# Extra yields ahead of the merge products and the convolution's transposes in a two-layer hybrid encoder

## The chip, the cores and the metric

One core of one Trainium2 chip runs the whole program. The metric is the device time of one execution in microseconds. The kernel before took 2913.32 us, the median of three runs (2912.23 to 2919.48).

## What is computed

The program is a two-layer encoder. In each layer a normalised input of 1024 positions is multiplied by one wide matrix `w_in`, and the columns of the product feed three mixers:

- a convolution module: a gated product of two column groups (256 channels), a depthwise convolution along the sequence, a layer norm over the channels, SiLU;
- differential attention: two softmax maps of queries and keys, one subtracted from the other, applied to values;
- a gated delta rule in two directions: queries, keys and values behind a short convolution, with a decay and a step size for each position. It is computed in chunks of 64 positions. In each chunk a unit lower triangular 64x64 matrix A, made of keys and decays, has to be inverted.

The results are merged by an output projection, and a feed-forward block follows. All products are held to fp32 accuracy: an operand is split into a high and a low part, and three matmuls stand for one product.

## The kernel before

**The phase that the change touches** is `w_in_phase` (L293). It multiplies by `w_in` in 21 steps of 128 columns each. A step (`dense_fm`) loads one weight tile (the DMA L177 on SP's queue), splits it (L168 on ACT, L169 on DVE), issues 2 x 8 x 3 = 48 matmuls (L163, L164, L165: the high and low parts), and evacuates the product by a function of its own (L425 to L429 for queries and keys of the attention, L440 for its values and for z). Both layers run this phase, from about 90 us and from about 1500 us in the trace.

**Work laid among the steps.** Two Python generators are advanced between the steps; each `yield` ends a portion of issued instructions. Behind every step, `prep` is advanced 8 times; from the moment that both inputs of the convolution exist, `conv_module` is advanced 6 times. This goes on until 5 steps are left (`LATE`); behind that the rest of both generators is issued, and the last 5 steps alternate with the delta rule's own products.

- `conv_module` (L485): the depthwise convolution on DVE (L508, L512: products over 31 taps for two halves of the channels, into the tiles `ca`), then for each quarter q of the sequence the transposes of `ca` on TensorE (L525), the layer norm's statistics on DVE, a power on POOL (L158, `lnro`), L530 on DVE, transposes back (L534), and SiLU on ACT (L537).
- `prep`: for each of the three head pairs p, `dn_a(p)` makes the chunk matrices A (transposes L674 and L718, decays L704 and L708 on POOL, the product L723 on DVE). It is advanced one portion for every two portions of `invert(p-1)`. What is left of `invert(p-1)` follows before `invert(p)` exists. At the end `prep_v` (L642 to L646) runs beside `invert(2)`.
- `invert(p)` (L762): A is taken as four 32x32 blocks. It loads the diagonal blocks (tiles `Lr` and `Lp`, DMAs L776, a transposing copy L777 on ACT), inverts them by 31 substitution steps on POOL (L787, L788 on the tile `Xm`), transposes the result on ACT (L790, `XT`), stores both to DRAM (L792, L793 on SP), loads them back as `Tt` and `Ta` (L801, L804: 12 DMAs on SP), yields once, and then issues the products that merge the blocks: 32 with `Ta` (L811, L812), an evacuation (L814), 32 with `Tt` (L819, L820), the evacuations L823 and L824 and the store L826 into `kta`, from which the delta rule reads (L859). `Lr` and `XT` share one pair of buffers, so that `Lr` of pair p+1 is allocated behind `XT` of pair p.

**What sets the order.** Nothing in the source fixes the order on an engine. A planner simulates the program while it is being built: it places each instruction on its engine (and each DMA on its queue) when its inputs are ready in that simulation, and among ready ones it takes the one that was issued first. So the place at which an instruction is issued is a priority. Evacuations and weight loads are issued with a priority that is higher by 1000 instructions. One step, with the portions of the generators that go with it, issues some 110 instructions, so this is about 9 steps. What the planner has fixed is the order on the chip; an engine there waits at an instruction whose input is late, and everything behind it waits too.

Steps 0 to 3 are two tiles for the delta rule and the two inputs of the convolution (each of twice the length); 4 to 8 are further tiles of the delta rule, 9 to 14 the queries and keys of the attention (q0, k0, q1, k1, q2, k2), 15 to 17 its values, 18 to 20 z.

Of the kernel before, what the change touches and what calls it, by code (L numbers as in the profile page):

```python
# [78 lines left out]
class K:  # L79
# [403 lines left out]
    def conv_module(self, l, L, W, up, dw, db, lw, lb):  # L483
        nc = self.nc
        cas = []  # L485
        for i in range(2):
            ca = W.tile([P, S], F32, tag="ca", bufs=2, name=f"ca{l}_{i}")
            u = up[i]

            H, M = S // 2, S // 2 + 15  # L490
            xe, xo = u[:, 0::2], u[:, 1::2]
            ye, yo = ca[:, 0::2], ca[:, 1::2]
            h0, h1 = dw[:, i, 0::2], dw[:, i, 1::2]
            hs = W.tile([P, 16], F32, tag="hs", bufs=2, name=f"hs{l}_{i}")
            nc.vector.tensor_tensor(hs[:, 0:15], h0[:, 0:15], h1, op=ALU.add)
            nc.vector.tensor_copy(hs[:, 15:16], h0[:, 15:16])
            x1 = W.tile([P, M], F32, tag="x1", bufs=1, name=f"x1_{l}_{i}")
            nc.vector.tensor_tensor(x1[:, 0:M - 1], xe[:, 1:M], xo[:, 0:M - 1], op=ALU.subtract)
            nc.vector.tensor_tensor(xe, xe, xo, op=ALU.subtract)
            yield  # L500
            nc.vector.tensor_scalar(yo, xo[:, 0:H], hs[:, 0:1], db[:, i:i + 1], ALU.mult, ALU.add)
            for k in range(1, 16):
                nc.vector.scalar_tensor_tensor(yo, xo[:, k:k + H], hs[:, k:k + 1], yo, ALU.mult, ALU.add)
                if k % 2:
                    yield
            nc.vector.scalar_tensor_tensor(ye, xe[:, 0:H], h0[:, 0:1], yo, ALU.mult, ALU.add)
            for k in range(1, 16):
                nc.vector.scalar_tensor_tensor(ye, xe[:, k:k + H], h0[:, k:k + 1], ye, ALU.mult, ALU.add)  # L508
                if k % 2:
                    yield  # L510
            for k in range(15):
                nc.vector.scalar_tensor_tensor(yo, x1[:, k:k + H], h1[:, k:k + 1], yo, ALU.mult, ALU.add)  # L512
                if k % 2:
                    yield
            cas.append(ca)
        for q in range(4):
            ps = self.bank("sc0", 1).rearrange("p (t k) -> p t k", k=CONV_CH)
            pa = self.bank("sc1", 1).rearrange("p (i t k) -> p i t k", i=2, k=P)
            xc = W.tile([P, 2, CONV_CH], F32, tag="lnx", bufs=2, name=f"lnx{l}_{q}")
            st = W.tile([P, 2, 6], F32, tag="lnst", bufs=2, name=f"lnst{l}_{q}")  # L520
            mv = W.tile([P, 2, 2], F32, tag="lnmv", bufs=2, name=f"lnmv{l}_{q}")
            for tt in range(2):
                t = 2 * q + tt
                for i in range(2):
                    nc.tensor.transpose(ps[:, tt, i * P:(i + 1) * P], cas[i][:, t * P:(t + 1) * P], self.ident)  # L525
                nc.vector.bn_stats(st[:, tt], ps[:, tt])
                nc.vector.bn_aggr(mv[:, tt], st[:, tt])
            r = self.rstd(W, mv[:, :, 1], 1.0, 1e-5, "lnr")
            for tt in range(2):
                nc.vector.tensor_scalar(xc[:, tt], ps[:, tt], mv[:, tt, 0:1], r[:, tt:tt + 1], ALU.subtract, ALU.mult)  # L530
            yield
            for i in range(2):
                for tt in range(2):
                    nc.tensor.transpose(pa[:, i, tt], xc[:, tt, i * P:(i + 1) * P], self.ident)  # L534
            yo = W.tile([P, 2, CONV_CH], F32, tag="lnx", bufs=2, name=f"yo{l}_{q}")
            for i in range(2):
                nc.scalar.activation(yo[:, i], pa[:, i].rearrange("p t k -> p (t k)"), AF.Silu, scale=lw[:, i:i + 1], bias=lb[:, i:i + 1])  # L537
                nc.scalar.dma_start(self.yd[i, :, q * CONV_CH:(q + 1) * CONV_CH], yo[:, i])
            yield
# [218 lines left out]
    def invert(self, l, p, A, X):  # L758
# [39 lines left out]
        for g in range(4):  # L798
# [3 lines left out]
                                  xi[1 - d, 64 * d + 16 * g:64 * d + 16 * g + 16].rearrange("m r c -> r m c"))  # L802
            d = g % 2
            nc.sync.dma_start(Ta[r], xi[d, 64 * d + 16 * g:64 * d + 16 * g + 16].rearrange("m r c -> r m c"))  # L804
        yield
        ps = self.dt_bank().rearrange("p (g c) -> p g c", c=B)
        Tf = [t.rearrange("p m h c -> p (m h) c") for t in Tt]
        for g in range(16):
# [826 lines left out]
```

## Time and profile before

| | |
|---|---|
| median of three runs | 2913.32 us |
| the profiled execution | 2917.9 us |
| its span in the trace | 2916.1 us |
| mean granted TensorE clock | 0.956 of full speed |
| TensorE matmuls (PE), busy | 2681.5 us, 92% |
| VectorE (DVE), busy | 2064.0 us, 71% |
| ScalarE (ACT), busy | 1404.8 us, 48% |
| GpSimd (POOL), busy | 842.7 us, 29% |

The profile is one execution, taken by the hardware profiler. Its span is 1.8 us under its own time, and its time is 4.6 us over the median of the runs. Engines are PE (TensorE matmul), PEld (its weight loads), DVE, ACT, POOL and SP; SPq is the DMA queue that SP issues. A name such as L525 is a line of the kernel. A row of the timeline gives start and duration in us, engine, line, operation, output<-inputs and shape, and in brackets the idle time of the engine just before and what ended it. Busy shares are means over stages with different limits.

### The profile page before, as it was taken

The numbers are of one execution on the slowest core, as the hardware profiler recorded it, in microseconds if no ns is written. First come the engines' busy times: TensorE is split into PE (matmuls) and PEld (weight loads), VectorE is DVE, ScalarE is ACT, GpSimd is POOL, SyncE is SP. The second block draws the span as 40 slices with busy tenths as digits, with TensorE's granted clock in tenths as the row PEclk, the third lists the DMA queues.
The fourth block names the chain that finished last, engine by engine and source line by source line (L and its number), as shares of the span: only waits on it lengthen the run. The fifth ranks groups of instructions, "written<-read, shape, count | busy, mean of one in ns | idle before, by whom it ended". The sixth has DMA issues, their size and how long they took to land.

```text
span 2916.1 us, 46184 instructions
## 1 busy us (share of the span) xinstructions
PE 2681.5 (92%) x17292; PEld 2155.4 (74%) x17292; DVE 2064.0 (71%) x3781; ACT 1404.8 (48%) x2468; POOL 842.7 (29%) x793
## 2 busy tenths in 40 slices
PE   8987989888999998999999879698889999989997
PEld 7865766666888886888787667476668888868886
DVE  5797247987488776777768871388874977757776
ACT  5433336586356664322554332276853566643224
POOL 2289636754100000000112985377530000000000
PEclk9998989989999999999999989799989999999999
DMA  5467795433235558655445496953332455586643
GB/s 133 151 172 210 219 225 145 117 102 123 87 105 216 206 192 314 233 202 184 150 118 146 142 265 170 224 150 107 109 121 75 145 196 206 212 336 209 220 169 116
DMA packets 415314, 504.76 MB, mean 173 GB/s; under 512 B 125401, under 2 KB 313945, under 8 KB 412786
## 3 DMA queue, kind: packets, MB, share of 16 engines
q1 hardware_dynamic: 359362, 373.92, 42.9%
q10 hardware_dynamic: 55728, 127.88, 11.5%
q8 instruction: 137, 2.24, 0.3%
q14 instruction: 87, 0.71, 0.1%
HBM read 318.01 MB, written 182.12 MB: 172 GB/s over the span
## 4 chain that ended last, share of the span: by engine, by line
PE 62%; POOL 11%; DMA 10%; DVE 8%; issue 4%; ACT 2%; SPq 2%; ACTq 0%; DVEq 0%; POOLq 0%
PE at L163 10%; PE at L164 10%; PE at L165 10%; PE sc L163 4%; PE sc L164 4%; PE sc L165 4%; POOL Xm L788 4%; POOL subt L787 3%; DVE sc L1070 3%; PE dt L163 2%; PE dt L164 2%; PE dt L165 2%; PE tr L163 2%; PE tr L164 2%; DMA qkT<-gq 2%
## 5 line engine op out<-in xcount | busy, mean ns | idle before, releaser
L158 POOL TENSOR_TENSOR pro<-pr,mhalf 128x1 f32<-128x1 f32 x32 | 18.5, 578 | 1417.8 <-DVE pr L207 1415.0
L163 PE MATMUL at<-hTh,wh 128*128 128x512 f32 (+1 forms) x832 | 326.8, 394 | 11.8 <-DVE qkl L426 8.0
L165 PE MATMUL at<-hTh,wl 128*128 128x512 f32 (+1 forms) x832 | 325.5, 392 | 5.4 <-DVE wl L169 5.4
L164 PE MATMUL at<-hTl,wh 128*128 128x512 f32 (+1 forms) x832 | 326.3, 392 | 0.0
L1073 ACT ACTIVATE sc<-sc,mx 128x1024 f32<-128x1024 f32 x192 | 220.2, 1149 | 94.3 <-DVE mx L1070 89.1
L163 PEld LDWEIGHTS at<-hTh,wh 128*128 128x128 f32 x832 | 160.3, 193 | 43.4 <-DVE qkl L426 8.5
L165 PEld LDWEIGHTS at<-hTh,wl 128*128 128x128 f32 x832 | 160.3, 193 | 37.2 <-DVE wl L169 6.2
L164 PEld LDWEIGHTS at<-hTl,wh 128*128 128x128 f32 x832 | 160.6, 193 | 31.0 <-issue 0.8
L1068 PE MATMUL at<-stk 96*128 96x512 f32 x352 | 153.7, 489 | 29.7 <-DVE mx L1070 27.9
L1070 DVE CUSTOM_DVE_ANT_0 sc<-at,bias 128x512 f32<-128x512 f32 x192 | 129.7, 684 | 43.0 <-PE at L1068 25.0
L1070 DVE CUSTOM_DVE_ANT_0 sc<-at,bias,mx 128x512 f32<-128x512 f32 x192 | 141.9, 745 | 19.6 <-PE at L1068 13.8
L1180 ACT ACTIVATE ob<-sb 128x512 fp32r<-128x512 f32 x120 | 74.8, 626 | 155.0 <-PE tr L165 54.8
L169 DVE TENSOR_TENSOR wl<-wr,wh 128x1024 fp32r<-128x1024 f32 x48 | 65.2, 1359 | 117.5 <-ACT wh L168 117.4
L787 POOL TENSOR_TENSOR subt<-Lp,Xm 128x31 f32<-128x31 f32 (+15 forms) x186 | 124.9, 672 | 70.9 <-DMA Lp<-ai 50.5
L163 PE MATMUL at<-ob,oa 128*128 128x512 f32 x356 | 138.4, 391 | 2.1 <-ACT at L1508 2.1
L164 PE MATMUL at<-ob,oa 128*128 128x512 f32 x356 | 138.6, 390 | 0.0
L165 PE MATMUL at<-ob,oa 128*128 128x512 f32 x356 | 138.0, 389 | 0.0
L788 POOL TENSOR_TENSOR Xm<-Xm,subt 128x31 f32<-128x31 f32 (+15 forms) x186 | 133.9, 720 | 12.9
L1094 PE MATMUL tr<-consts,sc 128*128 128x128 f32 x704 | 114.8, 296 | 15.3 <-DVE sc L1090 4.6
L1180 ACT ACTIVATE ob<-w2r 128x512 fp32r<-128x512 f32 x92 | 57.6, 629 | 130.7 <-PE tr L165 52.1
L1094 PEld LDWEIGHTS tr<-consts,sc 128*128 128x128 f32 x704 | 85.7, 150 | 36.9 <-issue 11.4
L1068 PEld LDWEIGHTS at<-stk 96*128 96x128 f32 x352 | 66.0, 203 | 61.2 <-DVE mx L1070 48.9
(469 smaller groups left out, 7940.2 us busy)
## 6 DMA issues: line engine op xcount, KB each, us to landing
hd<-oa ACTq DMA_DIRECT2D x120, 512.0 KB, 6.3
oa<-hd SPq DMA_DIRECT2D x120, 512.0 KB, 4.4
w1r<-in_w_ff_dram SPq DMA_DIRECT2D x32, 1024.0 KB, 5.6
w2r<-in_w_ff_dram SPq DMA_DIRECT2D x64, 512.0 KB, 7.1
wr<-in_w_in_dram SPq DMA_DIRECT2D x50, 512.0 KB, 4.8
ld<-hd SPq DMA_DIRECT2D x98, 256.0 KB, 3.9
kta<-kta SPq DMA_DIRECT2D x32, 576.0 KB, 9.9
stk<-qk SPq DMA_DIRECT2D x66, 256.0 KB, 5.0
```

The source lines that it names most:

```text
L158: self.nc.gpsimd.tensor_tensor(out, x, half[:, :n], op=ALU.pow)
L163: mm(ps, lhsT=lh, rhs=rh, start=first, stop=False, skip_group_check=more)
L164: mm(ps, lhsT=lh, rhs=rl, start=False, stop=False, skip_group_check=more)
L165: mm(ps, lhsT=ll, rhs=rh, start=False, stop=last, skip_group_check=more)
L169: (eng or self.nc.vector).tensor_tensor(lo, raw, hi.bitcast(F32), op=ALU.subtract)
L787: nc.gpsimd.tensor_tensor(tv, Lp[:, j + 1:, j:j + 1].broadcast_to([P, n, w]), Xm[:, j:j + 1, 0:w].broadcast_to([P, n, w]), op=ALU.mult)
L788: nc.gpsimd.tensor_tensor(Xm[:, j + 1:, 0:w], Xm[:, j + 1:, 0:w], tv, op=ALU.subtract)
L1068: mm(ps, lhsT=st[:, 0, t * P:(t + 1) * P], rhs=st[:, 1, ks], start=True, stop=True)
L1070: nc.vector.tensor_tensor_reduce(out=sc[:, ks], in0=ps, in1=self.bias[:, o:o + 512], scale=slope, scalar=mx[:, 0:1] if n2 else 3.0e38, op0 ...
L1073: nc.scalar.activation(sc, sc, AF.Exp, scale=-1.0, bias=mx[:, 1:2], accum_out=oS[:, t, mp:mp + 1])
L1094: nc.tensor.transpose(ps[:, k], pp[0][:, (4 * q + k) * P:(4 * q + k + 1) * P], self.ident)
L1180: self.nc.scalar.activation(h, src, AF.Copy)
```

## The change

Two generators that only set the order of issue get more `yield`s: six in the convolution module, ahead of the four quarters of transposes, and ten in place of one in `invert`, between the loads of `Tt` and `Ta` and the products that merge the blocks. No instruction is added, removed or altered.

```diff
@@ -513,6 +513,9 @@
                 if k % 2:
                     yield
             cas.append(ca)
+
+        for _ in range(6):
+            yield
         for q in range(4):
             ps = self.bank("sc0", 1).rearrange("p (t k) -> p t k", k=CONV_CH)
             pa = self.bank("sc1", 1).rearrange("p (i t k) -> p i t k", i=2, k=P)
@@ -802,7 +805,9 @@
                                   xi[1 - d, 64 * d + 16 * g:64 * d + 16 * g + 16].rearrange("m r c -> r m c"))
             d = g % 2
             nc.sync.dma_start(Ta[r], xi[d, 64 * d + 16 * g:64 * d + 16 * g + 16].rearrange("m r c -> r m c"))
-        yield
+
+        for _ in range(10):
+            yield
         ps = self.dt_bank().rearrange("p (g c) -> p g c", c=B)
         Tf = [t.rearrange("p m h c -> p (m h) c") for t in Tt]
         for g in range(16):
```

## Rows read from the trace of the kernel before

**Rows 1.** The page: busy time of each engine, and the chain's shares.

```profile
PE 2681.5 (92%) x17292; PEld 2155.4 (74%) x17292; DVE 2064.0 (71%) x3781; ACT 1404.8 (48%) x2468; POOL 842.7 (29%) x793
...
PE 62%; POOL 11%; DMA 10%; DVE 8%; issue 4%; ACT 2%; SPq 2%; ACTq 0%; DVEq 0%; POOLq 0%
```

**Rows 2.** PE's waits, layer 1's stage: line waited for: us, times, longest.

```profile
PE sc L859 <- DMA kta<-kta: 10.6, 2, 5.6
...
PE dt L811 <- DMA Ta<-xi: 8.8, 2, 8.4
PE sc L525 <- DVE ca L512: 7.9, 1, 7.9
...
PE dt L812 <- DMA Ta<-xi: 3.4, 1, 3.4
```

**Rows 3.** PE's waits, layer 0's stage (85 to 420 us).

```profile
PE dt L811 <- DMA Ta<-xi: 4.9, 2, 3.7
...
PE dt L812 <- DMA Ta<-xi: 1.4, 1, 1.4
PE sc L525 <- DVE ca L512: 1.0, 1, 1.0
```

**Rows 4.** PE's timeline, layer 1: the convolution's first transposes.

```profile
1701.88 0.27 PE L525 MATMUL sc<-consts,ca 128*128 128x128 f32 x1
...
1703.15 0.40 PE L165 MATMUL at<-hTh,wl 128*128 128x512 f32 x1
1711.47 0.47 PE L525 MATMUL sc<-consts,ca 128*128 128x128 f32 x1 [7.92 <-DVE ca L512]
```

**Rows 5.** Busy PE, PEld, DVE, ACT, POOL; granted clock, DMA share, GB/s.

```profile
1500.00:1840.00 340.00, 297.29 (x2183) 238.20 (x2181) 210.28 (x339) 120.46 (x152) 190.90 (x234) 0.94 0.64 182
1702.00:1712.00 10.00, 2.08 (x10) 1.47 (x9) 9.05 (x12) 0.88 (x2) 9.37 (x11) 0.69 0.13 20
1712.00:1719.00 7.00, 7.00 (x50) 5.25 (x49) 6.15 (x14) 2.45 (x4) 6.76 (x8) 0.71 0.76 236
```

**Rows 6.** The chain of waits in order of time, 1703 to 1726 us.

```profile
1711.47 0.47 PE sc L525
...
1717.33 6.12 DMA qk<-qkl
...
1723.47 0.95 POOL Tt L796
```

**Rows 7.** POOL's waits, layer 1, 1680 to 1810 us.

```profile
POOL Tt L796 <- DMA kta<-Tt: 0.7, 2, 0.5
```

**Rows 8.** ACT's timeline, layer 1: both later transposes XT, a value evacuation.

```profile
1743.44 2.11 ACT L790 ACTIVATE XT<-Xm 128x1024 f32<-128x1024 f32 x1 [4.28 <-POOL Xm L788]
...
1767.64 0.60 ACT L440 ACTIVATE vt<-at 128x512 f32<-128x512 f32 x1 [6.17 <-DMA Ta<-xi]
...
1800.02 2.13 ACT L790 ACTIVATE XT<-Xm 128x1024 f32<-128x1024 f32 x1 [4.35 <-POOL Xm L788]
```

**Rows 9.** SP's queue in order, layer 1, behind XT of pair 1.

```profile
1745.99 0.79 SPq L177 DMA_DIRECT2D wr<-in_w_in_dram  x1
1746.84 4.83 SPq L776 DMA_DIRECT2D Lr<-ai  x4
1751.77 1.29 SPq L646 DMA_DIRECT2D vs<-vs  x1
1753.67 0.34 SPq L434 DMA_DIRECT2D qk<-qkl  x1
...
1754.56 0.88 SPq L804 DMA_DIRECT2D Ta<-xi  x1
...
1760.77 0.91 SPq L804 DMA_DIRECT2D Ta<-xi  x1
```

**Rows 10.** POOL's timeline, layer 1: pair 1's last, pair 2's first substitution.

```profile
1743.16 0.25 POOL L788 TENSOR_TENSOR Xm<-Xm,subt 128x31 f32<-128x31 f32 x1
...
1757.32 0.25 POOL L787 TENSOR_TENSOR subt<-Lp,Xm 128x31 f32<-128x31 f32 x1 [6.14 <-DMA Ta<-xi]
```

**Rows 11.** PE's timeline, layer 1: the merge products of pair 1.

```profile
1759.39 0.39 PE L163 MATMUL at<-hTh,wh 128*128 128x512 f32 x1
1759.71 0.24 PE L811 MATMUL dt<-Ta,Ao 32*32 32x32 f32 x2
...
1767.18 0.23 PE L812 MATMUL dt<-Ta,Ao 32*32 32x32 f32 x1 [3.43 <-DMA Ta<-xi]
```

**Rows 12.** SP's waits, layer 1's stage.

```profile
SPq L177 <- DVE wl L169: 62.7, 12, 13.3
```

## The prediction

> **What bounds the kernel now.** I read the page first: TensorE (PE) is busy 92% of the span, and its products carry 62% of the chain of waits [rows 1]. So a gain must either take idle time out of PE, or shorten what PE waits for. Next I read PE's waits in the two stages that the change touches. In layer 1 the reader is to see three kinds: the convolution's transposes wait 7.9 us for DVE, the merge products 8.8 + 3.4 us for the tile Ta, and the delta rule's first products 10.6 us for kta, which is the merge's own result [rows 2]. Layer 0 has the same in small: 1.0, 4.9 and 1.4 us [rows 3]. These waits are what the change can reach: 7.9 + 1.0 = 8.9 us of transposes and 8.8 + 3.4 + 4.9 + 1.4 = 18.5 us of merges.
>
> Then I asked what the waits for Ta and kta hang on, by ACT's, SP's and POOL's timelines in layer 1. Pair 1's substitution ends on POOL at 1743.4 [rows 10], the transpose XT follows at once (1743.44) [rows 8], and SP's queue then runs nearly without a gap from a weight load at 1745.99 through Lr of pair 2 to the last Ta at 1760.77 [rows 9]. Pair 2's substitution starts at 1757.32, when Lr has come [rows 10], and ends with XT at 1800.02 [rows 8]. That is a second long chain beside PE: POOL is busy 190.90 of 340 us in the stage [rows 5], but inside a substitution it hardly waits: its one other wait that hangs on the merges, the clearing of Tt, is 0.7 us in two pieces [rows 7].
>
> **The change, part by part.** Nothing is added or removed, so every term is a change of order. The place of issue is a priority, and I counted yields to find the new places.
>
> *The ten yields in the inversion.* By count the merge of pair 1 is issued behind step 8 instead of step 6, that of pair 0 behind step 5 instead of 4, that of pair 2 behind step 13 instead of 9. On the chip, pair 1's merge runs at 1759 to 1767 us, single pairs among projection products [rows 11], beside the evacuation of a value tile at 1767.64 [rows 8]: that is step 15. The planner already puts it some seven steps behind its new place of issue, because it waits for readiness, not for its turn. A lower priority that is still higher than that of the neighbours changes nothing. So I cost the merges' move at nothing; what hides it is the lateness of Ta. Its bounds: below, a gain of all 18.5 us [rows 2, 3]; above, a loss through the queue (rival three). I take 0, since the row at 1759 to 1767 is the merge itself.
>
> With it, the loads behind the merges are issued later too: Lr of pair 1 and pair 2, and the twelve loads of Tt and Ta of each of these pairs. They are on SP's queue, and POOL's substitutions follow them. POOL has little else in its queue there; the decay products are issued by the same generator, which is delayed with them. I take 0 for these and keep rival three as the bound above.
>
> *The six yields in the convolution.* Here the move is real. In layer 1 the first transpose stands at 1701.88; the next one, for the second half of the channels, waits 7.92 us until 1711.47 [rows 4]. By count the first three quarters go from behind step 11 to behind step 12, the fourth from 12 to 13. One step is 48 products; some 42 of them now come ahead of that transpose, more than the 7.92 us need. The DVE products will be done, so this wait goes: 7.9 us in layer 1 and 1.0 in layer 0 [rows 2, 3]. The granted clock behind it was 0.71 in the next 7.00 us, in which PE was busy throughout [rows 5]; without the pause that costs nothing, another 7.00 x (1 - 0.71) = 2.0 us. PE stands 7.9 + 2.0 = 9.9 us ahead behind that place in layer 1.
>
> *Where the 9.9 us go.* The next thing PE meets that does not hang on PE is Ta of pair 1. Its last load is issued at 1760.77 behind a queue that starts with XT [rows 8, 9]. In that queue only one gap can be put down to a product of PE: the vs store ends at 1751.77 + 1.29 = 1753.06, and qk follows at 1753.67, so 0.6 us. On POOL the clearing of Tt may give its longest wait, 0.5 us [rows 7]. So Ta comes at most 0.6 + 0.5 = 1.1 us sooner, and of 9.9 us at least 8.8 turn into a longer wait in front of the merge products, 3.4 us now. Behind that XT of pair 2 at 1800.02 sets the second merge, and kta the delta rule, as before. I take the whole 1.1 us for layer 1; its bounds are 0 and 9.9. In layer 0 I take 0 of 1.0, since waits for Ta of 6.3 us follow there as well [rows 3].
>
> Late next, then, is Ta. What is queued behind the waiting merge on PE are projection products and the evacuations that need them: ACT's next evacuation already sat idle 6.17 us there [rows 8].
>
> **The sum.** Against the profiled execution: 2917.9 - 1.1 = 2916.8 us. That execution stands 4.6 us over the median, so by the median 2913.3 - 1.1 = 2912.2 us.
>
> *A rule against this.* Across the pause the granted clock was 0.69, and 0.71 behind it [rows 5]. The Trainium skill ("TensorE: Matmul & The Clock Gate", section "Why this matters for your kernels") says that a pause between bursts of matmuls puts TensorE back to the lower of its two clocks. The rows agree. By that rule a longer pause at the merge would cost the same 2.0 us there, and the sum would be 2914.2 us; my sum leaves this out, as the row of the present 3.43 us pause does not show its price.
>
> **Rivals.**
>
> *One: the conv wait is a gain to the end (faster).* The chain of waits itself runs through this transpose at 1711.47, the products behind it, the store of qk at 1717.33, and the clearing of Tt on POOL at 1723.47 [rows 6]. If that is a real link, the inversion moves forward with PE. Price: 7.9 + 1.0 + 2.0 = 10.9 us, 2902.4 us. Against it: POOL's wait at that place was no more than 0.5 us [rows 7], so the substitution was just as late by itself.
>
> *Two: the merges do move (faster).* If the planner's order puts further projection products ahead of the merge, the waits for Ta go as well: 18.5 + 10.9 = 29.4 us, 2883.9 us. For it: the waits are there. Against it: the merge sits seven steps behind its place of issue, and kta, waited for with 10.6 us, would come later by what the merge is put off.
>
> *Three: the loads lose their place on SP's queue (slower).* A weight load is issued with a priority about nine steps ahead of its step. Lr and Ta, issued some two to four steps later than now, may fall behind one more weight load, which waits for DVE to free its buffer: 62.7 us in 12 waits, 5.2 us each [rows 12]. It decides wherever a weight load without a free buffer is put in front of Lr or Ta, as one already stands in front of Lr at 1745.99 [rows 9]; the chain XT, Ta, merge, kta has no slack to take this up. The places are Lr and Ta of pair 2 in both layers. Two of the four give 10.4 us, 2923.7 us, all four 20.9 us, 2934.2 us. Against it: XT and its stores are planned when they are ready, and the queue behind XT at 1745.99 to 1760.77 is mostly the inversion's own.
>
> **How the numbers follow.** A measurement of this kernel can tell about 0.3%, 8.7 us, from no change. The forecast (the wait moves, 2912.2) gets 0.54: the rows give a limit for the gain on two engines. Rival one gets 0.20, as the chain speaks for it. Rival two gets 0.06. Rival three gets 0.20: any change of issue reshuffles the queue, and the inversion has no slack. Faster by over 0.3% is one and two, 0.26; within is the forecast, 0.54; slower is three, 0.20. The range reaches from rival one less 1.1 us, by which the lowest run shown stands under the median (2913.3 - 2912.2), so 2901.3, to rival three's two places with 2.0 us of clock lost at them, 2925.7. It leaves out rival two and the half of rival three with more than two places, 0.16.
>
> **What would show it.** Right: in layer 1 the wait of L525 for DVE is gone; the waits of L811 and L812 for Ta grow from 3.4 us at pair 1 to some 12; the stretch behind L525 has a clock near 1; XT of pair 2 stays at about 1800 us from the start, kta's wait near 10.6 us. Wrong, towards rival one: XT of pair 1 and of pair 2 come some 10 us sooner. Towards two: the merge stands behind more products, without a wait. Towards three: a weight load with a wait for DVE stands ahead of Lr or Ta, and XT of pair 2 comes later. If the planner moves other work (the attention's evacuations or the layer norm's power on POOL, say), the sum misses that, and the waits of PE by line would show it.

## The result, and the profile after

The changed kernel took 2944.84 us, the median of four runs (2942.86 to 2946.42), against 2914.94 of the kernel before (four runs): 1.0095 times as long, 95% interval 1.0079 to 1.0111. By this ratio 28 us are lost (the two medians lie 29.9 us apart); the forecast of 2912.2 and its range up to 2925.7 are missed. The profiled execution has a span of 2941.5 us, 25.4 over the span before.

The page of the changed kernel, engines and shares of the chain; in what follows line numbers of the changed kernel are 3 higher behind line 515, and 5 higher behind the second edit (L811 is now L816, L859 is L864):

```profile
PE 2686.3 (91%) x17292; PEld 2155.7 (73%) x17292; DVE 2072.7 (70%) x3781; ACT 1406.1 (48%) x2468; POOL 847.5 (29%) x793
...
PE 62%; POOL 12%; DMA 10%; DVE 9%; issue 3%; ACT 2%; SPq 2%; ACTq 0%; DVEq 0%; POOLq 0%
```

Beside [rows 1], PE's work grew by 4.8 us of 2681.5. The rest of the 25.4 us is waiting. To see where it arose, each instruction of PE was paired with the same one in the other trace (same line, same tiles, same occurrence). The table gives the median of the later start, in us, for stretches of 60 us of the kernel before; the other columns are runs of the section below, each against the same trace of before. One execution stands against one here, and executions of one kernel scatter: before_dn2 (below), at 1.0002 of the time before, ends 8.9 us late by the same pairing, and lr_hp's column is of the fastest of its twelve executions. So a single figure of a few us proves little; those of the changed kernel can be held against conv_only, and in layer 1 against both_l1.

```
start (before)  changed  conv_only  inv_only  both_l1  lr_hp  before_swap  before_lrswap  dnload_hp
  360 us         -1.9      -0.4       -0.3      1.4     2.3      2.4           1.2          1.3
  900 us          8.1       9.3        2.9      2.4     3.9     12.6           4.2         11.6
 1620 us         10.4       9.5        3.1      2.3     3.8     12.1           4.6         11.6
 1800 us         15.7      14.6        3.3      8.6    -0.4     11.8          15.7         18.9
 1860 us         22.2      23.8        2.6     16.2    -5.3      8.1          16.9         15.6
 2160 us         28.6      29.3        2.9     22.9     2.3     12.3          21.0         21.4
 2880 us         26.6      27.4        1.0     20.9     0.9     10.5          19.5         19.9
```

So the changed kernel loses 10.0 us in layer 0's attention (360 to 900), 5.3 in layer 1's inversion (to 1800) and 12.9 in the delta rule's first loads and layer 1's attention together (1800 to 2160). A row is the middle of 60 us, and the one at 1860 mixes these two: in stretches of 10 us PE is 15.7 us late at 1810, 29.2 at 1850, 16.4 at 1880 and 26.3 at 1910. Some 2 us more come once, at about 1140 us, and do not come in conv_only; some 2 us at 2580 go the other way in every column. Of these only the inversion lies in a stage of the yields; the attention of both layers is a phase that the edits do not touch.

**Layer 1's inversion.** PE's waits in the same stage (1500 to 1880 us), columns as in [rows 2]:

```profile
PE sc L864 <- DMA kta<-kta: 19.5, 2, 11.2
PE dt L816 <- DMA Ta<-xi: 12.3, 4, 9.8
PE tr L721 <- DVE Aqk L726: 7.2, 3, 5.4
PE at L1073 <- DMA stkE<-qk: 6.1, 1, 6.1
...
PE dt L817 <- DMA Ta<-xi: 1.1, 1, 1.1
```

The convolution's wait of 7.9 us is gone, as meant. In its place stands one of 5.4 us for another product of DVE, and kta is waited for 19.5 us in place of 10.6. Ta's waits are 13.4 us in all, 12.2 before. SP's queue says why kta is late; these rows answer to [rows 9]:

```profile
1754.74 0.32 SPq L796 DMA_DIRECT2D xi<-XT  x1
1755.11 4.24 SPq L779 DMA_DIRECT2D Lr<-ai  x3
1759.39 0.61 SPq L804 DMA_DIRECT2D Tt<-xi  x1
...
1763.57 0.49 SPq L779 DMA_DIRECT2D Lr<-ai  x1
```

Before, the four loads of Lr stood together and ahead of Tt and Ta. Now three stand there, and the fourth comes behind six loads of the pair before. The transposing copy on ACT needs all four, and POOL's substitution needs the copy. ACT and POOL, to set beside [rows 8, 10]:

```profile
1769.66 2.09 ACT L780 ACTIVATE Lp<-Lr 64x1024 f32<-64x1024 f32 x1 [1.57 <-DMA yd<-yo]
...
1814.46 2.12 ACT L793 ACTIVATE XT<-Xm 128x1024 f32<-128x1024 f32 x1 [8.76 <-POOL Xm L791]
```

```profile
1771.88 0.25 POOL L790 TENSOR_TENSOR subt<-Lp,Xm 128x31 f32<-128x31 f32 x1 [14.17 <-ACT Lp L780]
```

The substitution of pair 2 starts 14.56 us later than before (1757.32). XT of pair 1 was 9.15 us late already (1752.59 against 1743.44), so 5.4 are new; XT of pair 2 follows 14.44 later.

**The delta rule's first loads.** SP's queue behind that, first of the changed kernel, then of the kernel before:

```profile
1844.38 0.53 SPq L752 DMA_DIRECT2D kta<-kta  x1
...
1850.57 4.02 SPq L1043 DMA_DIRECT2D stk<-qk  x3
...
1856.88 0.35 SPq L752 DMA_DIRECT2D kta<-kta  x1
```

```profile
1828.66 0.52 SPq L749 DMA_DIRECT2D kta<-kta  x1
...
1835.05 0.58 SPq L749 DMA_DIRECT2D kta<-kta  x1
...
1840.47 1.47 SPq L1038 DMA_DIRECT2D stk<-qk  x3
```

The first kta load is 15.7 us later, as the whole stage is there. The second is 21.8 us later, because the attention's stk has gone ahead of it: 6 us, and PE, in order, waits for that one. But the exchange gives some of this back: the attention's first product then waits less for its own load stkE, 6.1 us (in the list of PE's waits above) against 9.5 before:

```profile
PE at L1068 <- DMA stkE<-qk: 9.5, 1, 9.5
```

Behind that wait PE is 16.4 us late (at 1880), little more than the 15.7 with which it came.

**Layer 0's attention.** POOL has two kinds of work there: it scales kta for the delta rule (L753 before, L756 after), and it adds two softmax maps for the attention (L1088 before, L1093 after), on which DVE, ACT and PE wait. POOL before, PE before, then POOL, DVE and PE of the changed kernel:

```profile
461.78 2.37 POOL L1088 TENSOR_TENSOR sc<-sc,sc 128x1024 f32<-128x1024 f32 x1
472.42 0.83 POOL L753 TENSOR_TENSOR kta<-kta,kw 128x384 f32<-128x384 f32 x1 [8.26 <-PE sc L859]
```

```profile
476.33 0.50 PE L1068 MATMUL at<-stk 96*128 96x512 f32 x1 [3.75 <-DVE mx L1070]
```

```profile
458.39 1.89 POOL L1092 TENSOR_TENSOR sc<-sc,cf 128x1024 f32<-128x1024 f32 x1 [0.20 <-DVE cf L1084]
473.55 0.83 POOL L756 TENSOR_TENSOR kta<-kta,kw 128x384 f32<-128x384 f32 x1 [13.27 <-DMA kta<-kta]
474.33 2.34 POOL L1093 TENSOR_TENSOR sc<-sc,sc 128x1024 f32<-128x1024 f32 x1
...
476.70 0.69 DVE L1075 CUSTOM_DVE_ANT_0 sc<-at,bias 128x512 f32<-128x512 f32 x1 [13.11 <-POOL sc L1093]
...
478.18 0.66 PE L858 MATMUL sc<-Sb,qkT 128*64 128x128 f32 x2 [10.66 <-DVE Sb L879]
```

Two neighbours on POOL have changed places. The scaling itself runs at nearly the same time in both, 472.42 and 473.55. Before, the addition is done ahead of it, at 461.78; now it stands behind, DVE is behind POOL and PE behind DVE, and PE is idle for 10.66 us, where it was idle for 3.75 before. Across this place (440 to 490 us, stretches of 10 us) PE falls back by 4.3 us, and by 5.1 in conv_only. The rest of the 10.0 us comes ahead of it (some 4 us, of which conv_only has 1) and behind it, up to 690 us; it was not traced to a single place.

**Layer 1's attention.** The same scaling waits there for a kta load that stands behind more of the attention's loads (issued at 1895.18 behind nine loads of stk, at 1871.32 behind six before), 18.29 us against 15.90, and PE's wait for POOL's addition has grown from 3.62 to 9.98. The kernel before, then the changed one:

```profile
1879.16 0.83 POOL L753 TENSOR_TENSOR kta<-kta,kw 128x384 f32<-128x384 f32 x1 [15.90 <-DMA kta<-kta]
...
1890.40 1.97 PE L1094 MATMUL tr<-consts,sc 128*128 128x128 f32 x8 [3.62 <-POOL sc L1088]
```

```profile
1904.74 0.83 POOL L756 TENSOR_TENSOR kta<-kta,kw 128x384 f32<-128x384 f32 x1 [18.29 <-DMA kta<-kta]
...
1914.29 1.97 PE L1099 MATMUL tr<-consts,sc 128*128 128x128 f32 x8 [9.98 <-POOL sc L1093]
```

### The profile page after: what moved, and what is told of

It reads as the page before. It is cut to its first block, busy times and chain, and to the rows that moved or that the text cites. A ratio compares the mean times of both kernels' runs of the same rounds, so it can differ in the third digit from the quotient of the medians.

```text
span 2941.5 us, 46164 instructions
## 1 busy us (share of the span) xinstructions
PE 2686.3 (91%) x17292; PEld 2155.7 (73%) x17292; DVE 2072.7 (70%) x3781; ACT 1406.1 (48%) x2468; POOL 847.5 (29%) x793
## 4 chain that ended last, share of the span: by engine, by line
PE 62%; POOL 12%; DMA 10%; DVE 9%; issue 3%; ACT 2%; SPq 2%; ACTq 0%; DVEq 0%; POOLq 0%
PE at L163 10%; PE at L164 10%; PE at L165 10%; POOL Xm L791 4%; PE sc L163 4%; PE sc L164 4%; PE sc L165 4%; POOL subt L790 4%; DVE sc L1075 3%; PE dt L163 2%; PE dt L164 2%; PE dt L165 2%; PE tr L163 2%; PE at L1073 2%; PE tr L164 2%
## 5 line engine op out<-in xcount | busy, mean ns | idle before, releaser
L1099 PE MATMUL tr<-consts,sc 128*128 128x128 f32 x704 | 115.5, 297 | 14.7 <-POOL sc L1093 10.0
```

Source lines behind the costliest of these rows:

```text
L1099: nc.tensor.transpose(ps[:, k], pp[0][:, (4 * q + k) * P:(4 * q + k + 1) * P], self.ident)
```

## The experiments

The theory after the result: the planner filled the queues otherwise, and a few places in them, each an instruction behind a transfer that lands later than its neighbours need, carry the 28 us. The rivals: the merges' lower priority carries it; or one common slowing does.

**Which edit, which layer.** conv_only keeps the six yields and has the inversion's one yield again; inv_only keeps the ten alone; both_l1 makes both edits depend on the layer:

```diff
-        for _ in range(6):
+        for _ in range(6 if l == 1 else 0):
             yield
...
-        for _ in range(10):
+        for _ in range(10 if l == 1 else 1):
             yield
```

> Only the six yields of the convolution; the inversion keeps its one yield. Theory: the whole loss comes through this edit, since the transposes that move let the queues be filled otherwise: about 2943 us, 28 over before, with the last Lr load of pair 2 behind loads of Tt and Ta in layer 1 and with POOL waiting some 13 us for kta in layer 0's attention. Rival: the ten yields of the inversion carry the loss (merges of lower priority, kta later): then this one is at 2915 or, with the transposes' wait of 7.9 us gone, below it.

Measured: 1.0072 (1.0057 to 1.0086), about 21 us by the ratio; its profiled execution took 2943.37 us, the second slowest of six, and its column in the table is close to the changed kernel's.

> Only the ten yields of the inversion. Theory: the merges are placed by readiness, so nothing moves that counts: 2915 us, within 5 of before, and PE still waits some 8 us for DVE at the convolution's transposes in layer 1. Rival: 2943 us, the loss is here.

Measured: 0.9995 (0.9984 to 1.0006). PE's waits between 1700 and 1900 us still have the old one:

```profile
PE sc L861 <- DMA kta<-kta: 11.2, 2, 5.6
PE at L1070 <- DMA stkE<-qk: 9.5, 1, 9.5
PE sc L525 <- DVE ca L512: 8.0, 1, 8.0
```

The ten yields in front of the merges do nothing that can be measured: the merges stand by readiness, and in the trace the whole order of DVE is that of before. Two moves on SP's queue are left; in layer 0 a weight load has gone ahead of two loads of Lp (at 200.62 us), and it costs nothing that can be measured. So the loss comes with the six yields in the convolution: some 21 of 28 us by themselves. The intervals of conv_only and the changed kernel just overlap, so it stays open whether the ten add anything on top of the six.

> Both edits, in layer 1 alone; layer 0 has the yields of before. Theory: the losses are separate places in the order: layer 0's 8 to 10 us (POOL waiting for kta) go, layer 1's 18 us (5 in the inversion, 6 in the loads of the delta rule, 7 in the attention) stay: about 2934 us. Rival: one common cause, so that the loss is all there, 2944, or all gone, 2915.

Measured: 1.0069 (1.0055 to 1.0084), some 20 us of 28, and 20.9 against 26.6 in the table's last row. Layer 0 is as before up to 900 us (2.4 where inv_only has 2.9), and layer 1 loses 18.6 us from 1620 to the end, 16.2 in the changed kernel. So the two layers lose separately.

**Lr put back in front, in the changed kernel.** The edit gives the higher priority to all loads of Lr and Lp, in all pairs and both layers, and to the copy on ACT:

```diff
-                nc.sync.dma_start(dst[64 * d + 16 * g:64 * d + 16 * g + 16], src)
-        nc.scalar.activation(Lp[0:64], Lr[0:64].rearrange("p a b -> p b a"), AF.Copy)
+                with self.tc.high_priority(offset=self.HP):
+                    nc.sync.dma_start(dst[64 * d + 16 * g:64 * d + 16 * g + 16], src)
+        with self.tc.high_priority(offset=self.HP):
+            nc.scalar.activation(Lp[0:64], Lr[0:64].rearrange("p a b -> p b a"), AF.Copy)
```

> The changed kernel with its loads of Lr and Lp and the transposing copy behind them issued at the higher priority that weight loads have. Theory: all four Lr loads stand ahead of Tt and Ta, pair 2's substitution starts some 10 us sooner than in the changed kernel, and the delta rule's kta load again stands ahead of the attention's stk: 5 + 6 us back in layer 1, 2933 us, and less where layer 0 gains as well. Rival: the place of Lr is only a mark of a stage that is late for another reason: pair 2's XT stays at 1814 us and the time at 2944.

Measured: 1.0020 (1.0008 to 1.0031), so 0.75% of the 0.95% is back, more than was expected. SP, ACT and POOL, each on a row of its own view:

```profile
1743.26 7.22 SPq L780 DMA_DIRECT2D Lr<-ai  x4
```

```profile
1799.78 2.13 ACT L795 ACTIVATE XT<-Xm 128x1024 f32<-128x1024 f32 x1 [5.38 <-POOL Xm L793]
```

```profile
1756.25 0.25 POOL L792 TENSOR_TENSOR subt<-Lp,Xm 128x31 f32<-128x31 f32 x1
```

All four loads stand ahead of Tt and Ta. The substitution starts 15.6 us sooner than in the changed kernel, of which 6.6 had been gained by XT of pair 1 (1746.01), and the second kta load is again ahead of stk, which brings PE's wait for kta down to 8.6 us. Layer 0's exchange on POOL has gone too: 3.9 in the table at 900 us. So the time that came back is not Lr's place in layer 1 alone. This execution, of 2917.19 us, was 8 us faster than the median of its kernel.

**The same places, one by one, in the kernel before.** `issue_after` keeps an instruction behind another on its queue. In both runs here the edit holds back one instruction, and the planner orders what follows anew: 192 of DVE's 3781 instructions in before_lrswap, 210 in before_swap and 37 and 13 of SP's 1117 loads and stores stand elsewhere than before (the fewest that must be taken out for the rest to agree). What is priced is thus a place with all that followed from it. before_lrswap holds back one of the 24 loads of Lr; `ta1` is the second Ta load of pair 1 in layer 1:

```diff
-                nc.sync.dma_start(dst[64 * d + 16 * g:64 * d + 16 * g + 16], src)
+                with self.tc.issue_after(self.ta1.ins) if (l, p, d, g) == (1, 2, 0, 3) else ExitStack():
+                    nc.sync.dma_start(dst[64 * d + 16 * g:64 * d + 16 * g + 16], src)
...
```

> The kernel before with one load held back, in layer 1: the last of the four Lr loads of pair 2 is issued behind the second Ta load of pair 1 at the earliest, and stands behind the fourth. Theory: pair 2's substitution starts 6 to 8 us later, its XT comes at 1806 to 1808 us, and the attention's stk loads then stand ahead of the delta rule's kta: plus 12 to 20 us in all, 2927 to 2935. Rival: the inversion has slack in front of the merge, and the time stays within 5 us of before.

Measured: 1.0052 (1.0036 to 1.0069), 15 us. The load is issued at 1764.33, XT comes at 1815.98, 11.5 us later when the 4.5 by which XT of pair 1 was late are taken off (1747.91 against 1743.44), which is more than the 6 to 8 expected. SP's queue, then ACT:

```profile
1764.33 0.95 SPq L777 DMA_DIRECT2D Lr<-ai  x1
```

```profile
1815.98 2.15 ACT L791 ACTIVATE XT<-Xm 128x1024 f32<-128x1024 f32 x1 [5.40 <-POOL Xm L789]
```

As foretold, stk goes ahead of kta:

```profile
1843.79 1.72 SPq L1041 DMA_DIRECT2D stk<-qk  x3
1847.16 0.58 SPq L749 DMA_DIRECT2D kta<-kta  x1
1853.50 0.58 SPq L749 DMA_DIRECT2D kta<-kta  x1
```

One late load of 64 KB, with what the planner then ordered otherwise, makes about half of the change's loss (10 to 20 of 28 us), without any yield.

before_swap makes the one exchange on POOL in layer 0 (`kd4` is the scaling of kta for the fifth pair of chunks):

```diff
...
-                    self.lastpool = nc.gpsimd.tensor_tensor(pp[0], pp[0], pp[1], op=ALU.add)
+                    with self.tc.issue_after(self.kd4.ins) if (l, h, t) == (0, 0, 6) else ExitStack():
+                        self.lastpool = nc.gpsimd.tensor_tensor(pp[0], pp[0], pp[1], op=ALU.add)
```

> The kernel before with one exchange on POOL, in layer 0's attention: one addition of two softmax maps (half of t = 6, head 0) is held behind the decay product on the kta tile of the fifth pair of chunks, as it stands in the changed kernel. Theory: POOL waits there some 10 us for kta's load, DVE and PE behind it: plus 6 to 9 us from about 480 us on, 2923 against 2915. Rival: that wait is hidden, and the changed kernel's loss in layer 0 comes of its other exchanges: within 2 us of before.

Measured: 1.0030 (1.0018 to 1.0042), 9 us. In the one trace 4.0 us of the lag at 490 us (10.2, in stretches of 10 us) arise at the exchange; 4.3 had come ahead of it (1.9 at 420, 6.2 at 430), where the order on POOL is still that of before. POOL, and then PE's wait (440 to 500 us), as in the changed kernel:

```profile
477.09 0.83 POOL L753 TENSOR_TENSOR kta<-kta,kw 128x384 f32<-128x384 f32 x1 [10.15 <-DMA kta<-kta]
477.88 2.34 POOL L1091 TENSOR_TENSOR sc<-sc,sc 128x1024 f32<-128x1024 f32 x1
```

```profile
PE sc L855 <- DVE Sb L876: 8.7, 2, 8.5
```

**stk put back behind kta, in the changed kernel.** dnload_hp issues the loads of the delta rule's first pair of chunks in layer 1 (qkT, eg, vs and kta) at the higher priority; Lr stays where the change put it.

```diff
-        for d in range(2):
-            c = slice(m[d] * P, m[d] * P + P)
+        with self.tc.high_priority(offset=1000 if l == 1 and o == 0 else 0):
+            for d in range(2):
+                c = slice(m[d] * P, m[d] * P + P)
...
```

> The changed kernel with the first loads of the delta rule in layer 1 (the first pair of chunks) at the higher priority, so that kta stands ahead of the attention's stk again; Lr stays behind Ta. Theory: pair 2's XT stays at 1814 us, the two waits of PE for kta fall from 19.5 to about 11, and 6 of the 28 us come back: 2939 against 2945. Rival: the attention's first loads then are what is late, PE's wait for stkE grows by as much, and the time stays at 2945.

Measured: 1.0056 (1.0039 to 1.0072), 11 us back where 6 were expected. XT stays late (1815.77), kta's waits fall to 13.9 us while stkE's grow from 6.1 to 7.6, and layer 1 loses 8.3 us from 1620 us to the end in place of 16.2. In stretches of 10 us its PE is 15.4 us late at 1880 and 14.7 at 1910, where the changed kernel has 16.4 and 26.3: the gain shows in the attention, behind the loads that were moved.

**Is anything left?** Both groups of loads at the higher priority, the inversion's and those of the delta rule's first three pairs, in both kernels, and each alone where it had not been tried. The edits are those of lr_hp and of dnload_hp, the latter with this condition, in both layers:

```diff
-        with self.tc.high_priority(offset=1000 if l == 1 and o == 0 else 0):
+        with self.tc.high_priority(offset=1000) if o <= 2 else ExitStack():
```

lr_dn2 is the changed kernel with both, before_lr_dn2 the kernel before with both, before_dn2 and before_lr_hp the kernel before with one, conv_lr_hp the six yields alone with Lr's.

> The changed kernel with two groups of loads at the higher priority: those of the inversion (Lr, Lp and the copy behind them) and the delta rule's own for its first three pairs of chunks, in both layers. Theory: with every queue place mended that was found, the change costs nothing: within 5 us of before, 2913 to 2922, and up to 8 us below if the transposes' wait that the change removed is a gain once the loads are in order. Rival: the loss has more places: 2925 or more.

Measured: 1.0034 (1.0021 to 1.0048).

> The kernel before with both groups of loads at the higher priority. Theory: within 5 us of before, and equal within 4 us to the changed kernel with the same two groups, since the yields then change no queue place that counts. Rival: the two differ by 8 us or more, so that the yields still act in some other place.

Measured: 1.0027 (1.0012 to 1.0041).

> The kernel before with the delta rule's loads for its first three pairs of chunks at the higher priority. It tells how much of a gain of the run above is the priority's own. Theory: these loads already stand in good order before, so within 4 us of it. Rival: the priority is a gain by itself, 5 us or more.

Measured: 1.0002 (0.9986 to 1.0018).

> The kernel before with the loads of Lr and Lp and the transposing copy at the higher priority. Theory: pair 2's substitution starts sooner by what SP's queue gives, XT of pair 2 in layer 1 comes 4 us sooner, and kta with it: up to 4 us in each layer, 2907 to 2915. Rival: other work moves against it, 2915 to 2920.

Measured: 1.0009 (1.0001 to 1.0018).

> Only the convolution's six yields, with the loads of the inversion at the higher priority. Theory: the inversion's ten yields do nothing, so this is the time of the changed kernel with the same priority, 1.002 times before, within 0.2%. Rival: they differ by 0.3% or more, and the ten yields count once Lr is early.

Measured: 1.0023 (1.0009 to 1.0038), as lr_hp: the ten yields do nothing here either.

lr_dn2 by itself speaks for its rival: 10 us over before, not 5. But the kernel before with the same two priorities is as slow; the two differ by 0.07%, well inside their intervals. So with these loads put ahead the yields cost nothing that can be measured, and they gain nothing either; the 0.3% is the price of the two priorities together. Lr's priority alone already brings the two kernels together: lr_hp at 1.0020 and before_lr_hp at 1.0009, with intervals that overlap. The orders of the two kernels still differ (47 of SP's loads and stores, 41 of POOL's 793 instructions), so it is not shown that these loads are the only places that count: two orders can also cost alike by chance. before_lr_hp falls short of its expected gain: in its trace pair 2's substitution brings kta sooner, but layer 0's attention is some 13 us later (that execution was the slowest of eleven, 7 us over their median). No version was faster than the kernel before.

## Why the prediction was wrong

- **The ten yields do nothing: right**, for the merges as for the loads behind them ("I take 0 for these"). inv_only is at 0.9995; in the changed kernel they still stand where Ta comes.
- **The convolution's wait goes: right.** L528 has no wait for DVE in either layer.
- **The 9.9 us are given back: right in size by luck, wrong in mechanism.** By the pairing of instructions PE is 10.6 us behind the old trace at 1700 us, 7.2 at 1730 and 10.0 again at 1790, so 0.6 is left of what was foretold as 1.1 at most. What takes most of it back is not Ta, whose waits from 1700 us on are 3.6 us (2.5 + 1.1) where some 12 had been foretold at pair 1, but DVE, which was busy for the whole of the pause and late with the chunk products too; its 9.05 of 10 us in the old pause [rows 5] spoke for that. PE's row, and the busy times and the granted clock (columns as in [rows 5]):

```profile
1723.66 2.63 PE L721 MATMUL tr<-kq 64*64 64x128 f32 x32 [5.36 <-DVE Aqk L726]
```

```profile
1718.00:1725.00 7.00, 1.64 (x18) 0.97 (x20) 7.00 (x13) 1.26 (x2) 6.39 (x8) 0.69 0.16 60
1725.00:1732.00 7.00, 7.00 (x47) 5.68 (x40) 5.98 (x13) 1.18 (x2) 6.68 (x9) 0.82 1.04 311
```

  The granted clock was 0.69 in the stretch of the new pause and 0.82 in the 7.00 us behind it, between the two levels of 1.2 and 2.4 GHz, where the old pause had 0.69 and 0.71 [rows 5]. The Trainium skill ("TensorE: Matmul & The Clock Gate", section "Why this matters for your kernels") has a pause put the engine back to the lower clock; the trace agrees, with 1.00 in the 6 us ahead of the pause. So the clock's loss went with the wait instead of away.
- **The step that failed: "Behind that XT of pair 2 at 1800.02 sets the second merge, and kta the delta rule, as before."** For the six yields in the convolution the sum had one effect, the transposes' wait, and let every queue behind it stand as it was: a change of order there was put at nothing without a reason. XT of pair 2 came at 1814.46, 5.3 us later than XT of pair 1 had already been, and kta's waits were 19.5 us in place of 10.6. One of the 24 Lr loads had lost its place, and then kta its place ahead of stk.
- **Rival three** had the engine, the load, the pair and the sign, with a chance of 0.20. It had the wrong cause: what overtook Lr was no weight load, but Tt and Ta of the pair before, and what moved it were the convolution's yields, not the inversion's. The weight load that it feared did pass two loads of Lp in layer 0, by the ten yields, without a cost that can be measured (inv_only). Its price of 5.2 us a place came from weight loads; before_lrswap puts one place in one layer, with all that followed from it, at 15 us. That XT, Ta, merge and kta have no slack was right: in before_lrswap XT's 11.5 us put PE back by 11.1 (4.6 in the table at 1620, 15.7 at 1800).
- **What no part of the sum held: the phases behind.** The sum ended with the stage that the yields are in. Some 10 us in layer 0's attention arise there, 4 to 5 of them where POOL takes the kta scaling ahead of the attention's addition, and most of the 12.9 us behind 1800 in layer 1 arise between 1880 and 2160, in the attention. The text named "other work" only as a thing to look for; it gave it neither a price nor a share in the range.

What stays open: why the planner's simulation, with the six yields, let the fourth Lr load fall behind, and why two instructions on POOL changed places 200 us later. The order is seen on the chip, and the price of two places was measured, each with the order that the planner made behind it; what the simulation held for ready at those moments was not examined. Layer 1's attention was not tried by itself: its cause is argued from the rows above and from dnload_hp alone. So is the split of the 28 us among the places, as every edit moved more than one of them.

## What to carry to other kernels

Where a planner orders the work, a change of issue order is not confined to what it moves: compare the order on each queue, also in later phases, and look for an instruction that now stands behind one that waits for a DMA. Price such a place by what stands behind the waiting instruction on its engine, not by the wait's own engine: POOL was busy 29% of the span, and one exchange on it, with what the planner then ordered otherwise, cost 9 us. An idle gap on PE that another engine's late work causes need not be gained by moving PE's part; here it came back at the next product of that engine.

## What was not expected of the hardware

Counted from XT of pair 1, the fourth Lr load of pair 2 was issued 3.4 us later than before (10.98 us behind XT, at 1763.57, against 7.57, at 1751.01), but the substitution on POOL that hangs on it began 5.4 us later (19.29 us behind XT against 13.88); POOL idled for 14.17 us there, 6.14 before. In between stands ACT, in order: the copy that needs all four loads came behind a weight split (1766.55 us) and an evacuation (1767.51) and began at 1769.66. Its row puts the last 1.57 us of ACT's idle time down to a store of ACT's own (yd), not to Lr. So here a late transfer cost POOL more than its own lateness, with a second in-order engine between them.

And a chain of three engines behind one load passed a wait on nearly whole: in layer 0's attention POOL was idle for 13.27 us, DVE for 13.11, PE for 10.66. In the kernel before, with one addition done ahead of the scaling, the same three were idle for 8.26, 5.18 and 3.75 us there.
